# In an attention kernel's software pipeline, the look-ahead score products are issued first in each slot

## The chip, the cores and the metric

The kernel runs on one core of a Trainium2 chip. The metric is the time of one execution in microseconds (us), measured on the device. PE is TensorE (its weight loads are shown apart as PEld), DVE is VectorE, ACT is ScalarE, POOL is GpSimd, and SP issues the DMAs.

## The reference, cut to what matters

One layer of a bidirectional encoder is applied to two sequences, "prompt" (1024 tokens) and "sample" (2048 tokens), of width 1024. For each sequence:

```
h = rms_norm(x); z = h @ w_in            # split into pool, q, k, v, memory queries and gates
pool_out = multiscale_pool(u_pool) * silu(g_pool)
attn_out = softmax(q k^T / 8) v * silu(g_attn)       # 8 query heads, 2 key/value heads of 64, q and k normed and rotated
x_out    = softmax(q_x k_m^T / 8) v_m * silu(g_x)    # 4 heads on 256 memory tokens
y = concat(pool_out, attn_out, x_out) @ w_out
out = x + rms_norm(y)
```

All is float32. The softmax subtracts the largest score of each query. The inputs' gains make the scores large, so that the subtraction is needed.

## The kernel before, in words

The first part of the program (up to about 700 us) makes the projections and writes q, k, v and the gates to DRAM. The second part makes the attention and the output projection, and the change lies there.

The second part goes over **pairs** of 128 queries (256 queries): the eight pairs of the sample first, then the four of the prompt. A pair has three **groups**, one for each of the two key/value heads (kinds 0 and 1) and one for the memory attention (kind 2). A group goes over its keys in chunks of 128: 16 for a sample head, 8 for a prompt head, 2 for the memory. One chunk is one **slot**. A sample pair so has 34 slots and a prompt pair 18. The loop at line 877 issues slot after slot, and on PE, DVE, ACT and POOL the instructions stand in just the order in which the loop issues them.

What a slot holds:

- **Scores**, `weights(k, j)` for j = 0 and 1 (L220, L224 for kind 2): two matmuls make 128 keys by 512 queries into one of two PSUM buffers S, and ACT takes the exponential (L227) into P. The largest score comes in through an extra row of the second operand, `qb`.
- **Sums**, `sums(k)` of the slot before (L239, L240): P is added to z. In the sample POOL adds the first half and DVE the second; in the prompt DVE adds all.
- **The look-ahead**, `largest(n)`: for a group that comes later, two matmuls (four in kind 2, L183) make 128 queries by 1024 scores into one of two PSUM buffers N (L191), and DVE takes their largest (L194, `nb` or `top`). After the last piece of a group, `shift` turns the results into the row of `qb` (L201, L128, and DMAs at L161 and L209). There is nearly always one look-ahead in a slot; the last slots have none.
- **Due work** at dictated slots, `due(slot)` in the middle and `due(slot + 0.5)` at the end: the values matmuls (L252) once for every four chunks; after a group's last chunk its totals (L260), which take one of the two N buffers, then `take` (L266, `o`) and the reciprocal (L272, `rz`), which frees that buffer; then the product with the gate on POOL (L288), the split for the output projection (ACT and POOL, L416) and the norm of the output (L383 and L386).
- **Fill**: the matmuls of the output projection of an earlier pair (L357 to L359), spread over the middle slots of a sample pair and the last ones of a prompt pair.

Call the slot of a group's first chunk its first slot. The totals of the group before stand at the end of the slot after it, `take` and the reciprocal one slot further. The buffers of N are given out in the order in which they came free: while the totals hold one, the N of the next two slots share the other, and the N of the third one gets the buffer that the reciprocal frees. The buffers that are given out are the same ones before and after the change.

The order of a slot in the kernel before (L879 to L911) is: S(k, 0); sums of k-1; loads; look-ahead N; `due(slot)`; S(k, 1); fill; `due(slot + 0.5)`.

Of the kernel before, what the change touches and what calls it, by code (L numbers as in the profile page):

```python
# [23 lines left out]
def encoder(ctx, tc, I, O):  # L24
# [385 lines left out]
    def at(slot, f, *args):  # L410

        later.setdefault(slot, []).append((f, args))

    def due(slot):
        for f, args in later.pop(slot, ()):
            f(*args)  # L416
# [36 lines left out]
    looks, n = {}, len(slots)  # L453
# [421 lines left out]
    with tc.manual_schedule(engines=order):  # L875
        slot = 0
        while slot < len(slots) or later or fill:
            g, k = slots[slot] if slot < len(slots) else (None, 0)
            if g:  # L879
                g.weights(k, 0)  # L880
            if 0 < slot <= len(slots):
                h, kh = slots[slot - 1]
                h.sums(kh)
            for x in loads.get(slot, ()):
                x.load()
            if slot in looks:
                looks[slot][0].largest(looks[slot][1])
            due(slot)
            if g:
                g.weights(k, 1)  # L890
            pauses = sum(x is None for x in fill)
            n = -(-(len(fill) - pauses) // max(1, until[0] - slot - pauses)) if fill else 0
            for _ in range(n):
                x = fill.pop(0)
                if x is None:
                    break
                out, h, c, start, final = x
                out.piece(h, c, start, final)
                if final:
                    if h == 0 and not out.last:  # L900

                        for n in sorted(later):
                            for x in [x for x in later[n] if x[0].__name__ in ("square", "norm", "out")]:
                                later[n].remove(x)
                                x[0](*x[1])
                    at(slot + END, out.half_out, h)
                    at(slot + 1 + END, out.square, h)
                    if h == 1:
                        at(slot + 2, out.norm)
                        at(slot + 3, out.out)  # L910
            due(slot + END)  # L911
            slot += 1
# [42 lines left out]
```

## Time and profile before

| | |
|---|---|
| time, median of 3 runs | 1884.9 us (1884.27 to 1885.07) |
| the profiled execution | 1885.1 us, of which the span of the instructions is 1883.0 us |
| PE busy | 1816.8 us, 96% |
| DVE busy | 1131.4 us, 60% |
| POOL busy | 856.7 us, 45% |
| ACT busy | 697.3 us, 37% |
| mean granted clock of PE | 0.991 |

Each row of a timeline gives the start in us from the span's first instruction, how long the instruction (or the run of like ones, "x2") took, the engine, the line of the kernel, the operation, what it writes and reads, and in brackets the idle time of the engine before it with what ended it. A row of waits reads: who waited for whom, us in total, how many times, the longest. The ends of matmuls are modelled: a matmul is shown for about 0.4 us, while two matmuls of 512 columns that follow each other start about 0.235 us apart, so the idle time shown before a matmul is less than the time lost by about 0.16 us. In the rows of windows, the granted clock of PE (1.00 is full speed) stands in front of the DMA share.

### The profile page before, as it was taken

Reading aid. Unit: us, or ns where it says so; the run is one execution under the profiler, and the core shown is the slowest. Engines: PE = TensorE matmul, PEld = TensorE weight load, DVE = VectorE, ACT = ScalarE, POOL = GpSimd, SP = SyncE. Lnnn points to the kernel's source line nnn. Section 1 sums busy time; section 2 is a strip of 40 time slices with the busy share of each in tenths; the row PEclk is TensorE's granted clock in tenths of the full one; section 3 lists DMA queues with packets and bytes.
Section 4 is the critical chain, followed back from the end, with each engine's and each line's share of the span. In section 5 each row is a group of like instructions: output and inputs, shape, how many; then the busy total and the mean of one; then the engine's idle time right before and its main releaser. Section 6 shows DMA issues by size and latency. Waiting matters only on the chain. (4 is left out here: it accounts for less than half of the span.)

```text
span 1883.0 us, 23531 instructions
## 1 busy us (share of the span) xinstructions
PE 1816.8 (96%) x8520; PEld 1282.0 (68%) x8520; DVE 1131.4 (60%) x1304; ACT 697.3 (37%) x1266; POOL 856.7 (45%) x756
## 2 busy tenths in 40 slices
PE   7999999999999998999999999999999999999996
PEld 6888888988988874465564656556565656565564
DVE  7755146431545167867768676767868576756743
ACT  5523233222422115434434343444434343433331
POOL 3665017520546008845638374664837461413313
PEclk9999999999999999999999999999999999999998
DMA  7634454254433926212122220212222242223211
GB/s 243 201 113 121 109 160 132 76 162 110 116 113 102 216 70 167 68 30 79 46 79 62 70 64 25 79 45 79 62 74 62 67 132 64 91 84 100 86 40 62
DMA packets 148485, 181.83 MB, mean 97 GB/s; under 512 B 21505, under 2 KB 118417, under 8 KB 148369
## 3 DMA queue, kind: packets, MB, share of 16 engines
q1 hardware_dynamic: 148368, 180.33, 33.6%
q8 instruction: 67, 1.10, 0.3%
q14 instruction: 50, 0.40, 0.1%
HBM read 126.50 MB, written 53.62 MB: 96 GB/s over the span
## 5 line engine op out<-in xcount | busy, mean ns | idle before, releaser
L227 ACT ACTIVATE P<-S 128x512 f32<-128x512 f32 x688 | 399.3, 598 | 558.3 <-PE S L220 436.2
L194 DVE TENSOR_REDUCE nb<-N 128x1 f32<-128x1024 f32 x256 | 311.6, 1218 | 240.3 <-PE N L191 239.5
L239 POOL TENSOR_TENSOR z<-z,P 128x512 f32<-128x512 f32 x224 | 316.9, 1415 | 223.7 <-ACT P L227 218.8
L252 PE MATMUL acc<-P,V 128*64 128x512 f32 (+1 forms) x1472 | 320.8, 578 | 0.5
L220 PE MATMUL S<-qa,KA 128*128 128x512 f32 x640 | 275.0, 430 | 9.2 <-ACT P L227 9.2
L240 DVE TENSOR_TENSOR z<-z,P 128x512 f32<-128x512 f32 (+1 forms) x272 | 273.6, 1006 | 12.7 <-ACT P L227 12.3
L63 POOL TENSOR_TENSOR rs<-rs,mhalf 128x1 f32<-128x1 f32 (+2 forms) x100 | 100.4, 1007 | 386.2 <-DVE rs L61 386.1
L220 PE MATMUL S<-qb,KB 65*128 65x512 f32 x640 | 254.5, 398 | 0.0
L548 PE MATMUL pz<-hT_hi,w_hi 128*128 128x512 f32 x592 | 233.2, 394 | 1.4 <-ACT vmst L806 0.8
L549 PE MATMUL pz<-hT_lo,w_hi 128*128 128x512 f32 x592 | 232.3, 392 | 0.0
L550 PE MATMUL pz<-hT_hi,w_lo 128*128 128x512 f32 x592 | 232.1, 392 | 0.2 <-DVE w_lo L69 0.2
L191 PE MATMUL N<-KA,qa 128*128 128x512 f32 x640 | 208.1, 406 | 18.4 <-DVE rz L272 11.7
L252 PEld LDWEIGHTS acc<-P,V 128*64 128x64 f32 x1472 | 98.6, 138 | 180.3 <-issue 171.2
L220 PEld LDWEIGHTS S<-qa,KA 128*128 128x128 f32 x640 | 120.4, 188 | 143.6 <-issue 72.5
L194 DVE TENSOR_REDUCE top<-N 128x1 f32<-128x1024 f32 (+1 forms) x88 | 107.0, 1218 | 96.7 <-PE N L191 76.9
L191 PEld LDWEIGHTS N<-KA,qa 128*128 128x128 f32 x640 | 116.9, 191 | 61.7 <-DVE nb L194 22.1
L548 PE MATMUL pz<-w_hi,hT_hi 128*128 128x384 f32 (+1 forms) x416 | 140.3, 338 | 1.4 <-ACT hT_hi L68 1.4
L549 PE MATMUL pz<-w_lo,hT_hi 128*128 128x384 f32 (+1 forms) x416 | 139.9, 336 | 1.0 <-DVE w_lo L69 0.9
L550 PE MATMUL pz<-w_hi,hT_lo 128*128 128x384 f32 (+1 forms) x416 | 140.1, 338 | 0.0
L357 PE MATMUL py<-wo_hi,mix 128*128 128x512 f32 x352 | 137.7, 391 | 0.0
L358 PE MATMUL py<-wo_lo,mix 128*128 128x512 f32 x352 | 137.6, 391 | 0.0
L359 PE MATMUL py<-wo_hi,mix 128*128 128x512 f32 x352 | 137.4, 390 | 0.0
(116 smaller groups left out, 2487.9 us busy)
## 6 DMA issues: line engine op xcount, KB each, us to landing
wraw<-w_in SPq DMA_DIRECT2D x15, 1536.0 KB
dg<-gst SPq DMA_DIRECT2D x48, 256.0 KB
qa<-dq SPq DMA_DIRECT2D x48, 256.0 KB
gz<-rows SPq DMA_DIRECT2D x72, 128.0 KB
x<-x_sample SPq DMA_DIRECT2D x16, 512.0 KB
xr<-x_sample SPq DMA_DIRECT2D x16, 512.0 KB
y_sample<-xr SPq DMA_DIRECT2D x16, 512.0 KB
dq<-qst SPq DMA_DIRECT2D x96, 64.0 KB
```

The lines of the kernel that those rows point to most:

```text
L191: nc.tensor.matmul(S[:, 512 * b:512 * b + 512], lhsT=q, rhs=KA[self.kind][:, k:k + 512], start=True, stop=True)
L194: nc.vector.tensor_reduce(out=out, in_=S, axis=AX.X, op=ALU.max, negate=True)
L220: nc.tensor.matmul(S, lhsT=K[self.kind][rows_, keys], rhs=q, start=n == 0, stop=n == 1)
L227: nc.scalar.activation(out=self.P[k][:, j], in_=S, func=AF.Exp)
L239: nc.gpsimd.tensor_tensor(out=z[:, :cut], in0=a[:, :cut], in1=P[:, :cut], op=ALU.add)
L240: nc.vector.tensor_tensor(out=z[:, cut:], in0=a[:, cut:], in1=P[:, cut:], op=ALU.add)
L252: nc.tensor.matmul(self.acc[64 * j:64 * j + 64, x], lhsT=v, rhs=P[:, j, x], start=(k, i) == (0, 0), stop=k == self.chunks - 1, skip_group_ ...
L357: nc.tensor.matmul(ps, lhsT=mh, rhs=wo_hi[:, c, cols], start=first, stop=False)
L358: nc.tensor.matmul(ps, lhsT=mh, rhs=wo_lo[:, c, cols], start=False, stop=False)
L548: nc.tensor.matmul(ps, lhsT=sh, rhs=mh, start=c == 0, stop=False)
L549: nc.tensor.matmul(ps, lhsT=sh, rhs=ml, start=False, stop=False)
L550: nc.tensor.matmul(ps, lhsT=sl, rhs=mh, start=False, stop=c == n - 1)
```

## The change

The look-ahead of a slot is issued at the slot's start: on PE its matmuls (N) stand in front of S(k, 0), where they stood behind it; on DVE its maximum stands in front of the sum of weights of the slot before, where it stood behind it. With it moves what `largest` issues after a group's last piece (L201, L128 on DVE and the DMAs of `qb`), and the loads of the slot are issued behind it.

```diff
         while slot < len(slots) or later or fill:
             g, k = slots[slot] if slot < len(slots) else (None, 0)
+            if slot in looks:
+                looks[slot][0].largest(looks[slot][1])
             if g:
                 g.weights(k, 0)
             if 0 < slot <= len(slots):
                 h, kh = slots[slot - 1]
                 h.sums(kh)
             for x in loads.get(slot, ()):
                 x.load()
-            if slot in looks:
-                looks[slot][0].largest(looks[slot][1])
             due(slot)
             if g:
                 g.weights(k, 1)
```

The order on ACT and on POOL is the same in both kernels. On SP a few DMAs change places. PE at the start of a sample pair, from the totals (L260) to the values of the first four chunks, before:

```order
L260 MATMUL N<-z,ones 32x256 x4
L220 MATMUL S<-qa,KA_5426 128x512
L220 MATMUL S<-qb,KB_5427 128x512
L191 MATMUL N<-KA_5428,qa 128x512 x2
L220 MATMUL S<-qa,KA_5426 128x512
L220 MATMUL S<-qb,KB_5427 128x512
L220 MATMUL S<-qa,KA_5426 128x512
L220 MATMUL S<-qb,KB_5427 128x512
L191 MATMUL N<-KA_5428,qa 128x512 x2
```

The same place after, as far as the second N behind the totals:

```order
L260 MATMUL N<-z,ones 32x256 x4
L191 MATMUL N<-KA_5428,qa 128x512 x2
L220 MATMUL S<-qa,KA_5426 128x512
L220 MATMUL S<-qb,KB_5427 128x512
L220 MATMUL S<-qa,KA_5426 128x512
L220 MATMUL S<-qb,KB_5427 128x512
L191 MATMUL N<-KA_5428,qa 128x512 x2
```

In each slot N has moved in front of the pair of matmuls that makes S(k, 0); the two S of a slot are now neighbours. DVE at the same place before, from the maxima (L194) of the two slots around the totals to the sums behind the reciprocal:

```order
L240 TENSOR_TENSOR z<-z,P 128x512
L194 TENSOR_REDUCE nb<-N 128x1 x2
L240 TENSOR_TENSOR z<-P 128x512
L194 TENSOR_REDUCE nb<-N 128x1
L266 TENSOR_TENSOR o<-acc,gate 128x512
L272 RECIPROCAL rz<-N 128x256
L240 TENSOR_TENSOR z<-z,P 128x512
L194 TENSOR_REDUCE nb<-N 128x1
```

And after:

```order
L240 TENSOR_TENSOR z<-z,P 128x512
L194 TENSOR_REDUCE nb<-N 128x1 x2
L240 TENSOR_TENSOR z<-P 128x512
L266 TENSOR_TENSOR o<-acc,gate 128x512
L272 RECIPROCAL rz<-N 128x256
L194 TENSOR_REDUCE nb<-N 128x1
L240 TENSOR_TENSOR z<-z,P 128x512
```

The first sum of the new group (z<-P) stood between two maxima; it now stands behind both and directly in front of `o` and the reciprocal. PE at the end of a prompt pair's fill, before:

```order
L359 MATMUL py<-wo_hi,mix 128x512
L220 MATMUL S<-qa,KA_5428 128x512
L220 MATMUL S<-qb,KB_6119 128x512
L191 MATMUL N<-KA_5426,qa 128x512 x2
L220 MATMUL S<-qa,KA_5428 128x512
L220 MATMUL S<-qb,KB_6119 128x512
L220 MATMUL S<-qa,KA_5428 128x512
```

And after:

```order
L359 MATMUL py<-wo_hi,mix 128x512
L191 MATMUL N<-KA_5426,qa 128x512 x2
L220 MATMUL S<-qa,KA_5428 128x512
L220 MATMUL S<-qb,KB_6119 128x512
L220 MATMUL S<-qa,KA_5428 128x512
L220 MATMUL S<-qb,KB_6119 128x512
L191 MATMUL N<-KA_5428,qa 128x512 x2
```

The N of the second slot stood behind that slot's S(k, 0) and now stands in front of it.

## The prediction

> **What bounds the kernel now.** I read the page first: the busy shares and the clock row.
>
> ```profile
> PE 1816.8 (96%) x8520; PEld 1282.0 (68%) x8520; DVE 1131.4 (60%) x1304; ACT 697.3 (37%) x1266; POOL 856.7 (45%) x756
> ```
>
> PE is busy for 96% of the span, so the end is PE's own work plus the time it waits. The change adds and removes no instruction, so only the waits, and the clock that they may cost, can move. The second view is the list of waits of PE over the part where slots run, split at the start of the prompt's pairs (the first three rows are for 690 to 1530 us, the last two for 1530 to 1883 us).
>
> ```profile
> PE N L191 <- DVE nb L194: 5.8, 16, 1.0
> PE N L191 <- DVE rz L272: 5.2, 9, 0.6
> PE S L220 <- ACT P L227: 4.6, 18, 0.3
> ...
> PE N L191 <- DVE rz L272: 6.5, 4, 2.0
> PE S L220 <- ACT P L227: 4.6, 13, 0.5
> ```
>
> The reader is to see how little there is to win: 27 us in these five rows. The waits of N on rz (the reciprocal) come once at each pair's start. The third view is the timeline of one such start, in a sample pair, with PE, DVE, ACT and POOL (columns: start, duration, engine, line, idle time before).
>
> ```profile
> 1122.64 0.50 PE L220 MATMUL S<-qa,KA 128*128 128x512 f32 x1
> 1123.21 0.63 PE L191 MATMUL N<-KA,qa 128*128 128x512 f32 x2
> 1124.24 0.64 PE L260 MATMUL N<-z,ones 128*32 128x256 f32 x8
> 1124.81 0.50 PE L220 MATMUL S<-qa,KA 128*128 128x512 f32 x1
> 1125.02 0.94 DVE L240 TENSOR_TENSOR z<-P 128x512 f32<-128x512 f32 x1
> 1125.38 0.63 PE L191 MATMUL N<-KA,qa 128*128 128x512 f32 x2
> 1126.05 1.23 DVE L194 TENSOR_REDUCE nb<-N 128x1 f32<-128x1024 f32 x1
> 1127.19 0.68 DVE L266 TENSOR_TENSOR o<-acc,gate 128x512 f32<-128x512 f32 x1
> 1127.33 0.72 PE L191 MATMUL N<-KA,qa 128*128 128x512 f32 x2 [0.32 <-DVE nb L194]
> 1127.79 1.75 DVE L272 RECIPROCAL rz<-N 128x256 f32<-128x256 f32 x1
> 1128.35 0.40 PE L220 MATMUL S<-qa,KA 128*128 128x512 f32 x1
> 1129.59 0.73 PE L191 MATMUL N<-KA,qa 128*128 128x512 f32 x2 [0.61 <-DVE rz L272]
> 1130.72 3.65 PE L252 MATMUL acc<-P,V 128*64 128x512 f32 x16
> ```
>
> Call the slots from 1122.64, 1124.81, 1126.32 and 1128.35 one to four. The totals (L260) take one of the two N buffers; the N of slots two and three then share the other, and the N of slot four waits for rz. Before that N stands S(k, 0), which PE makes while it would else wait. And DVE adds z<-P at 1125.02 while it waits for the N of slot two: it costs rz nothing there.
>
> **The change part by part.** *Pair starts.* With N in front, N of slot one starts at 1122.64, and N of slot two right behind the totals at 1124.81, 0.57 earlier. Its reduction began 0.67 behind N (1125.38 to 1126.05); the first pair of matmuls after the totals takes 0.11 longer (1124.81 to 1125.38 for one S, against 0.47 for two matmuls elsewhere), so it begins at 1125.59 and ends at 1126.81. N of slot three can be issued at 1126.32 and waits till about 1126.86: 0.54, as before. But z<-P now stands behind this reduction and ahead of o and rz. Without a competitor it takes 0.68 (the middle value of the row below), so o ends near 1128.0 and rz at 1129.68 instead of 1129.54. N of slot four starts at 1129.73 and now has both S of its slot behind it, where it had one: the values start at 1131.33, not 1130.72. That is +0.6, with PE idle for about 0.38 and 1.20 us instead of 0.32 and 0.61. Nine such starts stand in the first list, and one of the four in the second: 10 x 0.6 = +6.0 us.
>
> How long z takes hangs on POOL, as these rows show (all sample z on DVE: least, middle and longest in ns; then one that starts while POOL adds xr).
>
> ```profile
> L240 DVE TENSOR_TENSOR z<-z,P x168: 627/683/1800, 802.2 to 1446.8; 128x512 f32<-128x512 f32 x168
> 1105.79 2.77 POOL L386 TENSOR_TENSOR xr<-xr,y 128x1024 f32<-128x1024 f32 x1 [1.17 <-DVE y L383]
> 1107.37 1.74 DVE L240 TENSOR_TENSOR z<-z,P 128x512 f32<-128x512 f32 x1
> 1126.37 1.28 POOL L239 TENSOR_TENSOR z<-z,P 128x512 f32<-128x512 f32 x1 [0.96 <-ACT P L227]
> ```
>
> A z that meets a running POOL sum waits it out: 1.74 is 1.2 of POOL's rest and 0.6 of its own. At a pair start POOL's next z begins after the exponential of slot two, by my count 0.1 us behind DVE's z<-P, so I take 0.68; if POOL comes first, it is up to 1.28 more (a rival).
>
> *The clock after a pair start.* Windows at the same place of an earlier sample pair, and at the end of a prompt pair and behind it (columns: length, busy of PE, PEld, DVE, ACT, POOL, then the granted clock and DMA).
>
> ```profile
> 1017.60:1021.10 3.50, 2.58 (x11) 1.58 (x10) 3.50 (x5) 2.11 (x4) 2.63 (x3) 1.00 0.25 74
> ...
> 1703.70:1707.10 3.40, 2.16 (x11) 1.21 (x9) 2.12 (x3) 2.17 (x4) 3.40 (x3) 1.00 0.50 172
> 1707.10:1714.00 6.90, 5.60 (x14) 2.29 (x16) 6.87 (x7) 0.60 (x2) 0.10 (x1) 0.51 0.47 147
> ```
>
> With 0.92 us of idle PE in 3.5 the clock stays at 1.00; with 1.24 in 3.4 it falls to half for 6.9. A pair start after the change has 0.38 + 1.20 = 1.58 us of idle PE spread over 3.2. I estimate that it falls below in 3 of 10, since the idle time often splits between two stretches; each then costs about 1.5 us (3.4 us at half the clock is 1.7 lost, less what falls in the wait): +4.5, between 0 and 15. The Trainium skill ("TensorE: Matmul & The Clock Gate", Part 1, on the clock gate) says the clock halves after at least one idle window of about 3.4 us. The row of 1703.70 speaks against reading this as a wholly idle window, since PE was busy for 2.16 of it; by the rule this term would be nothing.
>
> *Prompt pair ends.* There rz follows o, and o waits for POOL (DVE, POOL and PE).
>
> ```profile
> 1703.51 1.21 DVE L194 TENSOR_REDUCE top<-N 128x4 f32<-128x1024 f32 x1
> 1704.67 2.52 POOL L416 TENSOR_TENSOR mix<-o,mix 128x512 fp32r<-128x512 f32 x2
> 1705.99 0.69 DVE L266 TENSOR_TENSOR o<-acc,gate 128x512 f32<-128x512 f32 x1 [1.28 <-POOL mix L416]
> 1708.40 1.22 PE L191 MATMUL N<-KA,qa 128*128 128x512 f32 x2 [1.96 <-DVE rz L272]
> ```
>
> z<-P fits into DVE's idle 1.28, so rz stays; the S that stood ahead of N now stands behind it, 0.47 at the full clock or 0.94 at half: 0.7 each. Three such places (6.5 in four waits, the longest 2.0): +2.1; if z delays POOL's mix, up to 3.5 each.
>
> *Slots that wait for ACT.* PE waits for exponentials in two patterns: the end of a prompt fill (first two rows) and sample slots behind casts of mix (last two).
>
> ```profile
> 1676.37 0.40 PE L220 MATMUL S<-qa,KA 128*128 128x512 f32 x1
> 1678.47 0.50 PE L220 MATMUL S<-qa,KA 128*128 128x512 f32 x1 [0.55 <-ACT P L227]
> ...
> 1104.96 1.14 ACT L416 CAST mix<-o 128x512 fp32r<-128x512 f32 x2
> 1106.65 0.50 PE L220 MATMUL S<-qa,KA 128*128 128x512 f32 x1 [0.32 <-ACT P L227]
> ```
>
> In the first, S(k, 0) waits and N stands behind it, though its buffer is free; in front, its 0.47 fills the wait: six of the thirteen waits, -2.8. In the second, S(k, 1) waits; its S(k, 0) comes 0.47 later from PE, so ACT starts its queue up to 0.3 later: 8 x 0.3 = +2.4.
>
> *Plain sample slots.* A slot without fill, from its N to the S of the slot after next:
>
> ```profile
> 1134.88 0.63 PE L191 MATMUL N<-KA,qa 128*128 128x512 f32 x2
> 1135.35 0.40 PE L220 MATMUL S<-qa,KA 128*128 128x512 f32 x1
> 1135.82 0.47 PE L220 MATMUL S<-qa,KA 128*128 128x512 f32 x1
> 1137.28 0.47 PE L220 MATMUL S<-qa,KA 128*128 128x512 f32 x1
> ```
>
> The two matmuls of N take 0.47, so the six of a slot 1.41, and the pitch is 1.46: S(k, 0) waits 0.05 or a little more for the exponential two ahead of it. The two S are now neighbours, and the second exponential queues behind the first (1.14 for two casts of the same shape against 0.47 of PE between the two S), so the wait goes to S(k, 1) and about keeps its size; over a run of four slots I count 0.06 more: four runs in eight pairs, +2.0 (-2 to +4).
>
> *Slots where N waits for nb.* The first matmul of four such slots, and the values behind them:
>
> ```profile
> 1112.34 0.50 PE L220 MATMUL S<-qa,KA 128*128 128x512 f32 x1
> ...
> 1119.05 3.65 PE L252 MATMUL acc<-P,V 128*64 128x512 f32 x16
> ```
>
> The 5.8 us in 16 waits are a backlog of DVE. Each N comes 0.47 earlier, and with it each reduction, but as many z stand between two reductions as before: 0. Bounds: none of it goes away, or the four slots (6.71 us) shrink to their PE work, 4 x 1.41 and 0.20 at the two changes to and from values, 5.84: -0.87 in eight pairs, -7. The z of the slot before a burst of values now waits in DVE's queue behind an nb that waits for PE; nobody reads it before the next totals, so it costs 0 here.
>
> SP: some loads of qb's row stand earlier in its queue; no wait of PE above is on them: 0.
>
> Sum: 6.0 + 4.5 + 2.1 - 2.8 + 2.4 + 2.0 = +14.2 us. The profiled execution took 1885.1 (span 1883.0 and 2.1 around it), the median of the runs is 0.2 less: 1884.9 + 14.2 = 1899.
>
> **The rivals.** *No clock drop:* the threshold lies above 1.58 us of idle PE. The sum loses 4.5: 1894.6. For it: 0.92 left the clock alone, and the idle time is in two pieces; against it: 1.24 did not, and in pieces too. The clock-gate rule of the Trainium skill ("TensorE: Matmul & The Clock Gate", Part 1), cited above, would give this case.
>
> *POOL goes first, and every pair start halves the clock:* z<-P costs 1.28 more, the idle rises to 2.8 us, well past 1.24. 10 x (0.6 + 1.3 + 1.5) + 3.7 (the other terms) = 38: 1923. It decides from 0.1 us of DVE's order against POOL's.
>
> *Faster:* the earlier reductions dissolve DVE's backlog (-7.0), N fills ACT's waits (-2.8), the clock holds, the plain slots come out at their lower end (-2.0), and the pair starts' +6.0 stay: -5.8, 1879. It decides if nb of the first slot after each burst keeps its 0.47 lead through POOL's interference. For it: nb holds N up sixteen times in the first list; against it: the z left from before the burst comes right behind.
>
> *No change:* each wait only moves to another row, as the plain slots do: 1885.
>
> **How the numbers follow.** Forecast 0.42, no clock drop 0.18, POOL first 0.14, no change 0.14, faster 0.12. About 0.2%, 3.8 us, is what a measurement can tell here. Slower by more: 0.42 + 0.18 + 0.14 less 0.02 for forecasts that come out small = 0.72; same 0.16; faster 0.12. The range 1880 to 1912 takes in the first two cases with their bounds (prompt ends up to 3.5 each, plain slots -2 to +4) and no change; it leaves out most of faster and of POOL first, some 0.2 together.
>
> **What would show it.** In the changed profile: N waiting for rz in ten sample-like starts with about 1.2 idle instead of 0.6; z<-P right behind the second of two nb there, at 0.68; some stretches at clock 0.50 before 1530 us; fewer waits of S on P after the prompt's fills. I am wrong if the waits on rz do not grow, or if those on nb vanish.

## The result: slower, by more than forecast

| | before | after |
|---|---|---|
| median | 1884.99 us (4 runs) | 1916.64 us (4 runs, 1911.50 to 1924.97) |
| ratio, 95% interval | | 1.0166 [1.0144, 1.0187] |
| the profiled execution | 1885.1 us, span 1883.0 | 1924.97 us, span 1923.2 |

The change costs 31.7 us; 14 were forecast. The direction was right, the size too small, and 1917 lies above the range. The profiled execution of after is the longest of its four, 8 us over the median, so its rows show the places better than the total.

### The profile page after: what moved, and what is told of

It is laid out like the page before. It is cut to its first block, busy times and chain, and to the rows that moved or that the text cites. A ratio compares the mean times of both kernels' runs of the same rounds, so it can differ in the third digit from the quotient of the medians.

```text
span 1923.2 us, 23537 instructions
## 1 busy us (share of the span) xinstructions
PE 1834.4 (95%) x8520; PEld 1290.4 (67%) x8520; DVE 1144.6 (60%) x1304; ACT 679.0 (35%) x1266; POOL 875.5 (46%) x756
## 5 line engine op out<-in xcount | busy, mean ns | idle before, releaser
L227 ACT ACTIVATE P<-S 128x512 f32<-128x512 f32 x688 | 379.1, 597 | 615.2 <-PE S L220 263.8
L194 DVE TENSOR_REDUCE nb<-N 128x1 f32<-128x1024 f32 x256 | 311.1, 1216 | 252.5 <-PE N L191 252.1
L239 POOL TENSOR_TENSOR z<-z,P 128x512 f32<-128x512 f32 x224 | 350.4, 1564 | 229.1 <-ACT P L227 224.3
L252 PE MATMUL acc<-P,V 128*64 128x512 f32 (+1 forms) x1472 | 325.0, 585 | 1.5 <-DVE o L266 1.5
L220 PE MATMUL S<-qa,KA 128*128 128x512 f32 x640 | 267.1, 417 | 15.2 <-ACT P L227 14.8
L240 DVE TENSOR_TENSOR z<-z,P 128x512 f32<-128x512 f32 (+1 forms) x272 | 268.3, 986 | 11.1 <-ACT P L227 10.5
L63 POOL TENSOR_TENSOR rs<-rs,mhalf 128x1 f32<-128x1 f32 (+2 forms) x100 | 95.3, 956 | 389.6 <-DVE rs L61 389.6
L191 PE MATMUL N<-KA,qa 128*128 128x512 f32 x640 | 221.9, 428 | 28.4 <-DVE rz L272 17.7
L191 PEld LDWEIGHTS N<-KA,qa 128*128 128x128 f32 x640 | 108.3, 191 | 142.0 <-issue 61.9
L194 DVE TENSOR_REDUCE top<-N 128x1 f32<-128x1024 f32 (+1 forms) x88 | 107.2, 1218 | 116.3 <-PE N L191 86.8
L357 PE MATMUL py<-wo_hi,mix 128*128 128x512 f32 x352 | 137.9, 392 | 0.0
L220 PEld LDWEIGHTS S<-qb,KB 65*128 65x128 f32 x640 | 124.2, 194 | 20.0
```

The lines of the kernel that those rows point to most:

```text
L191: nc.tensor.matmul(S[:, 512 * b:512 * b + 512], lhsT=q, rhs=KA[self.kind][:, k:k + 512], start=True, stop=True)
L194: nc.vector.tensor_reduce(out=out, in_=S, axis=AX.X, op=ALU.max, negate=True)
L220: nc.tensor.matmul(S, lhsT=K[self.kind][rows_, keys], rhs=q, start=n == 0, stop=n == 1)
L227: nc.scalar.activation(out=self.P[k][:, j], in_=S, func=AF.Exp)
L239: nc.gpsimd.tensor_tensor(out=z[:, :cut], in0=a[:, :cut], in1=P[:, :cut], op=ALU.add)
L240: nc.vector.tensor_tensor(out=z[:, cut:], in0=a[:, cut:], in1=P[:, cut:], op=ALU.add)
```

## The profile after

The page's row of busy shares: PE has as many instructions as before, and 17.6 us more of busy time (1816.8 before), the same work, longer where the clock is lower (its mean is 0.983 in this execution and 0.991 in that of before).

```profile
PE 1834.4 (95%) x8520; PEld 1290.4 (67%) x8520; DVE 1144.6 (60%) x1304; ACT 679.0 (35%) x1266; POOL 875.5 (46%) x756
```

Waits of PE in the seven sample pairs between about 780 and 1550 us (total, times, longest), first before, then after:

```profile
PE N L191 <- DVE nb L194: 4.3, 13, 0.4
PE N L191 <- DVE rz L272: 4.2, 7, 0.6
PE S L220 <- ACT P L227: 4.2, 16, 0.3
```

```profile
PE N L191 <- DVE nb L194: 9.2, 24, 0.5
PE N L191 <- DVE rz L272: 8.4, 7, 1.2
PE S L220 <- ACT P L227: 7.6, 15, 0.8
PE acc L252 <- DVE o L266: 1.5, 6, 0.3
```

The reader is to see that all rows have grown, not the one on rz alone: nb by 4.9, rz by 4.2, ACT by 3.4, and a new one on `o`, 1.5: 14.0 us, 2.0 a pair. Now the prompt's pairs between 1570 and 1840 us, before and after:

```profile
PE N L191 <- DVE rz L272: 5.9, 3, 2.0
PE S L220 <- ACT P L227: 4.0, 11, 0.5
```

```profile
PE N L260 <- DVE z L240: 8.6, 3, 2.9
PE N L191 <- DVE rz L272: 6.9, 4, 1.7
PE S L220 <- ACT P L227: 2.4, 5, 0.7
```

The row that heads the second list was not forecast: at each of three prompt pair ends the totals wait 2.9 us for the last sum. First the place that was forecast, a sample pair's start, in the timeline of after:

```profile
1139.16 0.68 DVE L240 TENSOR_TENSOR z<-P 128x512 f32<-128x512 f32 x1
1139.27 1.72 POOL L239 TENSOR_TENSOR z<-z,P 128x512 f32<-128x512 f32 x1 [0.94 <-ACT P L227]
1139.30 0.73 PE L191 MATMUL N<-KA,qa 128*128 128x512 f32 x2 [0.38 <-DVE nb L194]
1139.76 0.68 DVE L266 TENSOR_TENSOR o<-acc,gate 128x512 f32<-128x512 f32 x1
...
1142.17 0.74 PE L191 MATMUL N<-KA,qa 128*128 128x512 f32 x2 [1.20 <-DVE rz L272]
```

The sum z<-P stands in front of `o` and is 0.11 us ahead of POOL's; PE waits 0.38 and 1.20, as forecast. And a prompt pair's end, which was not:

```profile
1652.39 2.29 DVE L383 SCALAR_TENSOR_TENSOR y<-y,rs,npost 128x1024 f32<-128x1024 f32 x1
1654.60 1.21 DVE L194 TENSOR_REDUCE top<-N 128x1 f32<-128x1024 f32 x1
1654.81 2.35 POOL L386 TENSOR_TENSOR xr<-xr,y 128x1024 f32<-128x1024 f32 x1 [1.22 <-ACT P L227]
1655.73 2.51 DVE L240 TENSOR_TENSOR z<-z,P 128x1024 f32<-128x1024 f32 x1
1658.39 1.08 PE L260 MATMUL N<-z,ones 128*32 128x256 f32 x8 [2.86 <-DVE z L240]
```

DVE is late by the product of the norm (L383); the maximum then goes first, and the last sum, which the totals need, comes behind it and runs beside POOL for 2.51 us instead of 1.2. The windows of after (length, busy of PE, PEld, DVE, ACT, POOL, then the granted clock and DMA): the first inside a sample pair, behind waits of 0.79 us on ACT and 0.46 on nb, the others around this prompt end:

```profile
1231.70:1235.10 3.40, 3.40 (x10) 1.29 (x10) 3.33 (x4) 1.20 (x2) 3.40 (x4) 0.50 0.38 154
1655.00:1658.40 3.40, 0.54 (x4) 0.14 (x4) 3.40 (x3) 0.91 (x2) 3.40 (x2) 0.99 0.11 47
1658.40:1661.70 3.30, 3.30 (x15) 2.21 (x16) 1.98 (x2) 0.15 (x1) 3.30 (x3) 0.50 0.50 187
1665.20:1672.00 6.80, 6.63 (x16) 3.06 (x18) 4.78 (x6) 1.19 (x2) 1.27 (x1) 0.50 0.21 65
```

PE is idle for 2.9 us at the prompt's pair end, and then has half the clock, twice.

## The experiments

Two questions: where does the loss sit, and what makes it? Theory A was the prediction's own: DVE's moved sum at the pair ends and starts, the idle time of PE that it makes, and the clock. Rival B: N in front on PE makes the loss everywhere. In the table each median stands beside that of the kernel before on the same chip; "both" are the two halves of the change. The ratio is that of the means of the runs.

| run | median | before | ratio, 95% interval |
|---|---|---|---|
| 1 PE's half alone | 1907.41 | 1884.59 | 1.0128 [1.0112, 1.0144] |
| 2 DVE's half alone | 1928.18 | 1884.59 | 1.0228 [1.0212, 1.0244] |
| 3 both, in the sample only | 1907.48 | 1884.59 | 1.0120 [1.0100, 1.0139] |
| 4 both, a group's last sum first | 1913.30 | 1884.59 | 1.0161 [1.0142, 1.0180] |
| 5 both, first and last sum first | 1911.01 | 1886.13 | 1.0142 [1.0122, 1.0163] |
| 6 both, PE kept busy | 1908.44 | 1884.29 | 1.0130 [1.0115, 1.0145] |
| 7 before, PE kept busy at three prompt ends | 1876.22 | 1884.29 | 0.9963 [0.9948, 0.9977] |
| 8 both, old order at the prompt's pair ends | 1914.61 | 1884.29 | 1.0152 [1.0132, 1.0173] |
| 9 both, old order at all pair ends | 1901.67 | 1884.29 | 1.0094 [1.0079, 1.0110] |
| 10 before, kept busy at more places, one of them wrong | 1879.29 | 1886.13 | 0.9970 [0.9958, 0.9983] |
| 11 as 9, DVE's half only | 1912.04 | 1886.13 | 1.0141 [1.0124, 1.0157] |
| 12 as 9, PE's half only | 1901.54 | 1886.13 | 1.0082 [1.0066, 1.0099] |
| 13 as 12, N behind S after values | 1898.18 | 1884.22 | 1.0071 [1.0054, 1.0088] |
| 14 as 11, sum in front of `o` | 1889.84 | 1884.22 | 1.0033 [1.0022, 1.0044] |
| 15 before, kept busy, place mended | 1874.91 | 1884.22 | 0.9951 [0.9940, 0.9963] |
| 16 as 9, casts late | 1898.60 | 1884.90 | 1.0075 [1.0063, 1.0087] |
| 17 as 16, sum in front of `o` | 1901.44 | 1884.90 | 1.0083 [1.0069, 1.0096] |
| 18 before, casts late | 1886.11 | 1884.90 | 1.0003 [0.9993, 1.0013] |

### Each half alone (1, 2), and the sample alone (3)

In run 1 `largest` is split into its matmuls and, as `maximum`, the reduction and what follows, and only the matmuls move. Run 2 puts the whole call behind S(k, 0) and in front of the sum, so that on PE the order stays and on DVE the reduction moves. Both are shown against the kernel before:

```diff
 # run 1
+            if slot in looks:
+                look = looks[slot][0].largest(looks[slot][1])
             if g:
                 g.weights(k, 0)
...
             if slot in looks:
-                looks[slot][0].largest(looks[slot][1])
+                looks[slot][0].maximum(*look)
             due(slot)
 # run 2
             if g:
                 g.weights(k, 0)
+            if slot in looks:
+                looks[slot][0].largest(looks[slot][1])
             if 0 < slot <= len(slots):
...
-            if slot in looks:
-                looks[slot][0].largest(looks[slot][1])
             due(slot)
```

Run 3 makes the change only in slots that belong to a sample pair.

> Only PE's half of the change: the N matmuls in front of S(k, 0), while DVE keeps the sum of weights in front of the maximum. Theory A (DVE's half does most: the first sum of a group delays the reciprocal, and the last sum of a group delays the totals in the prompt): the totals of the prompt pairs no longer wait, the reciprocal at pair starts ends as in the kernel before, and only the S that now stands behind N costs, about 0.4 at ten pair starts, with the slots that wait for ACT: 1890 to 1900 us. Theory B (PE's half does most: N at the head of the slot blocks both S behind it): near the changed kernel, 1910 to 1918.

> Only DVE's half: the maximum in front of the sum of weights of the slot before, PE's order as in the kernel before. Theory A: most of the loss stays, with totals of the prompt pairs that wait for the last sum (about 3 us idle in each of three places) and half the clock behind them: 1903 to 1915 us. Theory B: close to the kernel before, 1885 to 1892.

> The whole change, but only in the slots of the eight sample pairs; the prompt's slots are issued as before. By the alignment of slots in the two traces a sample pair loses 2.4 us without a fall of the clock and about 1.6 more with one; theory A: 8 x 2.4 and two or three falls, 1905 to 1910 us. If the prompt pairs carry most of the loss (a rival), under 1900.

Run 1 fell between the theories, run 2 above both: +22.8 and +43.6 us, where the two together cost 31.7. The halves do not add. Alone, DVE's half is the worse one, and N in front makes it milder; why was not tested (PE's waits on rz and `o` in the seven sample pairs are 15.2 us in run 2 and 9.9 in the changed kernel). As the only cause theory B falls, but PE's half alone costs 22.8 us, and DVE's half on top of it only 9 more. Run 3 came as expected: 22.9 us of the loss are the sample's, which leaves some 9 to the prompt.

### One sum back in front (4), two (5)

```diff
+            h, kh = slots[slot - 1] if 0 < slot <= len(slots) else (None, 0)
+            ahead_sum = h is not None and (kh == h.chunks - 1)    # run 5: (kh == h.chunks - 1 or kh == 1)
+            if ahead_sum:
+                h.sums(kh)
             if slot in looks:
                 looks[slot][0].largest(looks[slot][1])
...
-            if 0 < slot <= len(slots):
-                h, kh = slots[slot - 1]
+            if h is not None and not ahead_sum:
                 h.sums(kh)
```

> The changed kernel, but the sum of a group's last chunk is issued in front of the maximum, so that the totals do not wait for it behind that maximum. Theory A: the wait of the totals on DVE's last sum (10.0 us idle in four places of the changed kernel) goes, and with it the half clock behind it; about 12 us less than the changed kernel: 1902 to 1908 us. Rival (the wait moves on to the reciprocal, which is late for POOL's sake anyway): less than 4 us less, 1912 to 1918.

> The changed kernel, but on DVE the sum of a group's first two chunks and the sum of its last chunk stand in front of the maximum again, as before; PE's order is the changed one. Theory A (at a sample pair's start the loss is the sum that stands between the second maximum and the reciprocal): the N that waits for rz waits 0.6 instead of 1.2 us, about 6 us come back, and the half clock behind the pair starts goes: 1903 to 1910 us. Theory B (with N in front on PE the wait only passes to the N of the slot before, which waits for its maximum, as the run with PE's part alone showed with 0.8 there): 1909 to 1916, as with the last sum alone in front.

Run 4 stayed with the rival. Its waits of PE behind 1530 us, and DVE at a prompt pair's end:

```profile
PE N L260 <- DVE top L194: 4.4, 3, 1.5
```

```profile
1648.35 1.21 DVE L240 TENSOR_TENSOR z<-z,P 128x1024 f32<-128x1024 f32 x1
...
1649.48 2.34 DVE L194 TENSOR_REDUCE top<-N 128x1 f32<-128x1024 f32 x2
...
1650.75 0.64 PE L260 MATMUL N<-z,ones 128*32 128x256 f32 x8 [1.47 <-DVE top L194]
```

The time is in the rival's range, though not by its wait: that on rz hardly changes (6.9 to 6.7 us in all). The sum is early now, and the totals wait for the buffer that the maxima free, up to 1.5 us where they waited 2.9 for the sum. Changing the order of the last two alone halves the wait and gives it another name. The rest may come of the sums that stood over from the slots before, which leave DVE an operation behind; that was not tested. Run 5, with the first sum in front too, followed its theory B. Its waits in the sample:

```profile
PE N L191 <- DVE nb L194: 14.2, 23, 1.2
...
PE N L191 <- DVE rz L272: 4.2, 7, 0.6
```

What the pair starts no longer lose to rz (8.4 to 4.2) they lose to nb (9.2 to 14.2).

### The order of before at the pair ends (8, 9)

```diff
+    behind = set()
+    for n, pair in enumerate(pairs[:-1]):
+        if 8 <= n < 99:                              # run 9: if 0 <= n < 99
+            end = max(first[g] + g.chunks for g in pair.groups)
+            behind.update(range(end + -1, end + 5))
...
-            if slot in looks:
+            if slot in looks and slot not in behind:
                 looks[slot][0].largest(looks[slot][1])
...
                 x.load()
+            if slot in looks and slot in behind:
+                looks[slot][0].largest(looks[slot][1])
             due(slot)
```

> The changed kernel, but with the order of before (on PE and DVE) in six slots around the end of each pair from the ninth on: the last slot of the pair and the five behind it. Theory A (the prompt loses because at a pair's end the moved sum stands behind a maximum that waits for PE, and with the product of the norm and POOL's additions comes too late for the totals; a matter of these slots alone): the totals no longer wait 2.9 us, the clock falls less there, and 3 x 3.2 us and some of the half clock come back: 1901 to 1907. Theory B (DVE runs late through the whole prompt since N stands in front): the totals go on waiting, 1911 to 1918.

> As the run before, but in these six slots of all pairs, the sample's too. Theory A (the loss of the change sits at the pair ends and starts: 0.6 us and the halved clock at each sample start, the totals in the prompt; what is left are about 1.1 us in each sample pair in the slots before its end and behind the casts): 1890 to 1898 us. Theory B (the loss is spread over the slots; a slot that waits less hands its loss on): 1900 to 1912.

What is left of the totals' waits between 1570 and 1840 us in run 8, in the list of waits:

```profile
PE N L260 <- DVE top L194: 1.0, 3, 0.3
```

The 2.9 us are gone (0.3 at the longest), as theory A of run 8 has it. Its time is less plain: the profiled run took 1907.06, the edge of A's range, the three others 1914.16 to 1915.38, B's, with a mean clock of 0.991 and 0.986. So how much these three places return can't be read from it. Run 9, in all pairs, is clear: 17.4 us above before. Some 14 of the 31.7 us sit in six of the 34 (or 18) slots of a pair, and the rest, 17, elsewhere: theory A's 1890 to 1898 is missed by 4 us, B's range holds it.

### What is left: each half inside the pairs (11, 12), and its cause (13, 14)

Runs 11 and 12 are run 9 with one half each in the other slots. Run 14 adds to 11, and run 13 to 12, one line:

```diff
 # run 14: the slot of each group's take
+    behind.update(n + g.chunks + 2 for g, n in first.items())
 # run 13: the first slot behind each burst of values
+    behind.update(n for n, (g, k) in enumerate(slots) if k % RUN == 1)
```

> Outside the six slots around each pair's end only DVE's half of the change (maximum in front of the sum); in these six slots, and on PE everywhere, the order of before. Theory A (what is left of the loss with the old order at the pair ends, 17 us, comes from PE's half: the two S of a slot are neighbours, and the second one waits for an exponential behind the casts of mix and behind the values): 1885 to 1890 us. Theory B (it comes from DVE's half): 1896 to 1904.

> The counterpart: outside the six slots around each pair's end only PE's half (N in front of the scores); in these six slots, and on DVE everywhere, the order of before. Theory A (PE's half makes what is left): 1896 to 1903 us, as with both halves. Theory B (DVE's half makes it): 1885 to 1890.

> The run with DVE's half alone outside the pair ends (1912.0 us, 26 above the kernel before), but in the slot of each group's take (o) the sum stands in front of the maximum again. Theory A (in the sample, o of the memory group is made a sum later, and the values that wait for its accumulator lose 0.7 us): in each of eight sample pairs 0.7 us comes back, and PE no longer waits 4.5 us in all on o; the prompt's loss, which goes by the product of the norm and POOL to ACT, stays: 1904 to 1909 us. Theory B (the wait on o only replaced another one): 1910 to 1914.

> The run with PE's half alone outside the pair ends (1901.5 us, 15 above the kernel before), but in the first slot behind each burst of values N stands behind S(k, 0) again. Theory A (PE's half loses because, behind a burst, ACT gets its first exponential 0.45 us later, the time of N's two matmuls, and has no slack to make it up in the four slots of a run once casts of mix stand between the exponentials): the waits on ACT shrink to those of before, and the loss of some 1.2 us in each sample pair goes: 1886 to 1892 us. Theory B (the loss comes of N in front in any slot, since the two S are neighbours everywhere): 1896 to 1903.

Theory A on runs 11 and 12 was right on the second and wrong on the first, which lies above both of its ranges: DVE's half alone costs 25.9 us there, PE's half 15.4, both 17.4. Two places in the profile of run 11 say how. The first stands in its list of waits in the sample; the others are a timeline in the prompt.

```profile
PE acc L252 <- DVE o L266: 4.5, 6, 0.8
```

```profile
1612.32 1.23 DVE L194 TENSOR_REDUCE top<-N 128x1 f32<-128x1024 f32 x1 [0.93 <-PE N L191]
1613.46 1.22 DVE L240 TENSOR_TENSOR z<-P 128x1024 f32<-128x1024 f32 x1
1614.60 0.68 DVE L266 TENSOR_TENSOR o<-acc,gate 128x512 f32<-128x512 f32 x1
...
1617.61 2.38 POOL L386 TENSOR_TENSOR xr<-xr,y 128x1024 f32<-128x1024 f32 x1 [1.45 <-issue]
...
1620.03 0.59 ACT L365 COPY y<-py 128x512 f32<-128x512 f32 x1 [6.65 <-POOL xr L386]
...
1621.16 0.50 PE L220 MATMUL S<-qa,KA 128*128 128x512 f32 x1 [1.54 <-ACT P L227]
```

DVE stands idle 0.93 us for N, with a sum queued behind; then the sum takes its 1.2 us in front of `o` and of the norm's product (L383), POOL's addition comes late, ACT's copy of y waits for that, an exponential stands behind the copy, and PE waits 1.54 us for it. In the sample the values wait for `o` itself (0.8). Run 14 puts the sum back in front in this slot alone: 1889.84, at least 14 us below what theory A forecast, which had counted on the sample's place only; both are mended. There the sum runs in the time in which DVE waits:

```profile
1601.48 1.22 DVE L240 TENSOR_TENSOR z<-P 128x1024 f32<-128x1024 f32 x1
1602.62 1.22 DVE L194 TENSOR_REDUCE top<-N 128x1 f32<-128x1024 f32 x1
1603.75 0.68 DVE L266 TENSOR_TENSOR o<-acc,gate 128x512 f32<-128x512 f32 x1
```

So nearly all that DVE's half costs alone is located: with the old order at the pair ends and in this slot 5.6 us are left of the 43.6 of run 2.

PE's half is not. Run 13, 1898.18 us (1893.22 to 1903.29), lies in theory B's range, and its interval overlaps that of run 12; the waits on ACT stayed at 7.3 us in 15, where run 12 has 7.5 and before 4.2, so a late first exponential behind the values is not their cause.

### The casts (16, 17, 18)

```diff
-        at(slot + 1 + END, nc.scalar.copy, hi, a)
+        at(int(slot + END) + 1 + END, nc.scalar.copy, hi, a)
```

> The changed kernel with the old order in six slots around each pair's end (1901.7 us, 17 above the kernel before), and on ACT the casts of the attention's products (mix<-o) stand behind a slot's second exponential, where they stood between its two. Theory C (with N in front, the two S of a slot and so their exponentials are neighbours, and ACT's gap lies behind the second one; a cast between the two has no gap to fall into, which makes the waits on ACT of 10.2 us against 4.2 before): some 0.4 us comes back at each such cast, two in a sample pair, and the waits on ACT fall towards 5: 1893 to 1898 us. Theory D (ACT lacks time for the cast wherever it stands): 1900 to 1904.

> As the run before, and also the old order in the slot of each group's take. Both halves of the change stay in the other slots. Theory C, with the sum standing in front of o again: another 1.5 us of waits on o and some 0.5 us in each prompt pair come back: 1888 to 1895 us. If it gets below the kernel before, N in front is worth something in plain slots; theory C gives no reason for that.

> The kernel before with only these casts moved behind the slot's second exponential. Theory C: with N between the two S, the gap lies between the two exponentials, so the move takes the cast out of its gap and costs 0.2 to 0.4 us at some of sixteen places in the sample: 1886 to 1891. Theory D: the place of the cast does not matter: 1882 to 1886.

Waits of PE between 780 and 1550 us in run 9, then in run 16:

```profile
PE S L220 <- ACT P L227: 9.4, 22, 0.8
PE N L191 <- DVE nb L194: 8.7, 24, 0.4
```

```profile
PE N L191 <- DVE nb L194: 14.3, 22, 1.5
...
PE S L220 <- ACT P L227: 2.7, 9, 0.7
```

The waits on ACT do go with the casts' place (9.4 to 2.7), but 5.6 of those 6.7 us come back as waits for nb, and the time hardly moves (1901.67 to 1898.60). That is a little above theory C's range and below D's. Run 17, with `o` mended too, is no better and misses its range: the waits on `o` (1.6 us in run 16) are gone, and those on nb have grown from 14.3 to 16.9. In the order of before the place of the casts makes no difference that can be measured (run 18, interval across 1; its median lies where the two ranges meet). A slot that waits less for ACT hands its loss to N.

One place shows this row by row: in a sample pair, the four slots ahead of the last values of the second head. PE's waits there in the kernel before, in run 12 (whose line numbers from the reduction on are three higher) and in run 16:

```profile
1214.23 0.50 PE L220 MATMUL S<-qa,KA 128*128 128x512 f32 x1 [0.22 <-ACT P L227]
...
1215.75 0.50 PE L220 MATMUL S<-qa,KA 128*128 128x512 f32 x1 [0.32 <-ACT P L227]
```

```profile
1228.19 0.50 PE L223 MATMUL S<-qa,KA 128*128 128x512 f32 x1 [0.79 <-ACT P L230]
...
1229.31 0.73 PE L191 MATMUL N<-KA,qa 128*128 128x512 f32 x2 [0.38 <-DVE nb L197]
```

```profile
1226.55 0.73 PE L191 MATMUL N<-KA,qa 128*128 128x512 f32 x2 [1.48 <-DVE nb L194]
```

From values to values these slots take 10.57 us before (1207.28 to 1217.85), 11.25 in run 12 (1219.66 to 1230.91) and 11.30 in run 16 (1216.83 to 1228.13). The place of the casts decides whom PE waits for; the 0.7 us are lost either way. In the other six sample pairs from the second on run 12 takes 11.2 to 12.3 us there and the kernel before 10.6. What makes PE's half cost some 15 us inside the pairs stays open; the runs show only that it is no single one of these waits.

### PE kept busy while it waits (6, 7, 10, 15)

Matmuls into a PSUM tile that nobody reads, ahead of an instruction that would wait (run 7; run 6 has them in the changed kernel, five at seven sample starts, and twelve and seven at the prompt's ends):

```diff
+    idle = {}
+
+    def keep_busy(count):
+        pad = pso.tile([128, 512], F32, name="py", tag="py")
+        for _ in range(count):
+            nc.tensor.matmul(pad, lhsT=wo_hi[:, 0, 0:128], rhs=wo_hi[:, 1, 0:512], start=True, stop=True)
+
+    for pair in pairs[8:-1]:
+        end = max(first[g] + g.chunks for g in pair.groups)
+        idle[end + 3], idle[end + 4] = 2, 8
...
+            if slot in idle:
+                keep_busy(idle[slot])
             if slot in looks:
```

> The changed kernel with matmuls that nobody reads (five ahead of the N that waits for rz in seven sample pair starts; twelve ahead of the totals and seven ahead of that N at the prompt's pair ends), 0.235 us each, put where PE would stand idle, so that it is busy while it waits. No output changes. Theory A (part of the loss is the halved clock, and the clock halves because PE stands idle for more than about 1.2 us in 3.4): the stretches at half clock behind these places are gone, and with them 1.7 us for each of some three in the sample and up to 3.4 us for each of the prompt's; 1898 to 1908 us. Theory B (the clock falls by something else, or the waits alone make the loss): the stretches stay and the time is that of the changed kernel or a little more, 1912 to 1920.

> The kernel before with two and eight such matmuls ahead of N in the two slots of three prompt pair ends in which N waits for rz (2.0 us each). No output changes. Theory A (the idle PE halves the clock for 6.8 us there, which costs up to 3.4 us each): 1874 to 1881 us, faster than the kernel before. Theory B (the matmuls only push the work behind them): 1885 to 1892.

> The kernel before with the unread matmuls of the earlier run at three prompt pair ends, and further ones at the three other places where PE stands idle and the clock then halves: thirteen ahead of the first totals of the program (3.3 us of waiting), six ahead of the last totals and seven ahead of the last output projection. No output changes. Theory A (idle PE is what halves the clock): no stretch at half clock is left between 740 us and the last matmul; against the run with the first three places another 3.4 us at the first and 1.7 us at the tail are saved: 1869 to 1874 us. Theory B: the first and the last places are held up by transfers and POOL anyway, 1875 to 1878.

> The kernel before with the unread matmuls at three prompt pair ends and at the tail, and thirteen now ahead of the totals that wait 3.3 us for POOL at 753 us (the earlier run had put them ahead of the first totals of the program, where PE does not wait, so they cost 3 us there). No output changes. Theory A (idle PE halves the clock): no half clock is left between 740 us and the last matmul: 1870 to 1875 us. Theory B (POOL holds the totals, and the work behind them, anyway): 1875 to 1878.

Run 7 at a prompt pair end, timeline and window; the prediction shows the same place of before, with 1.96 us of waiting and a clock of 0.51 behind it:

```profile
1703.99 2.00 PE L880 MATMUL py<-wo_hi 128*128 128x512 f32 x8
1706.11 0.72 PE L191 MATMUL N<-KA,qa 128*128 128x512 f32 x2
```

```profile
1703.00:1710.00 7.00, 6.88 (x32) 3.86 (x33) 6.26 (x7) 1.69 (x3) 1.92 (x2) 1.00 0.44 153
```

N starts 7.0 us behind the totals of the group before it, as in the kernel before, and the clock holds: theory A, and 7 to 8 us under the kernel before (by the means and by the medians). Run 6 shows the same in the changed kernel: at a prompt pair's end the totals still come late, but at full clock,

```profile
1646.00:1653.00 7.00, 6.28 (x33) 4.18 (x32) 6.18 (x4) 2.28 (x4) 5.78 (x4) 1.00 0.18 75
```

and the ratio is 1.0130 against 1.0166 of the changed kernel (the median is 0.4 us above theory A's range): filling the waits returns some 7 us. That is not the clock's share of the 31.7. The same remedy returns as much in the kernel before, whose clock falls too, and on one chip the two filled kernels are 32.2 us apart (1908.44 and 1876.22), no less than the two unfilled ones. How much of the 31.7 us comes from added falls of the clock stays open. In run 10, which lies above both of its ranges, thirteen of these matmuls stood ahead of the wrong totals, where PE does not wait; in the trace the work behind them comes 3 us later, which is their own time (13 x 0.235). In run 15 they stand where PE waits 3.3 us for POOL: 1874.91, in theory A's range and the fastest of all the kernels, though against run 7 the intervals overlap.

## Why the prediction was wrong

- **The failed step: the slots inside the pairs.** The prediction gave them +2.0 (plain slots), 0 (slots that wait for nb), -2.8 and +2.4 (waits on ACT), 1.6 us together. With the old order at all pair ends they cost 17.4 (run 9), and this is nearly the whole miss: the pair ends got 12.6 with the clock, and run 9 returns 14.3. Inside the pairs PE's half alone costs 15.4 (run 12). N now stands in front of both S of its slot, and PE's waits for nb in the seven sample pairs go from 4.3 to 9.7 us, outside the bounds that the prediction gave them, nothing and -7; those on ACT go from 4.2 to 7.5. The two rows make 8.7 of the 15.4; why they grow so, and the rest, stay open.
- **A second wrong step** is a sentence: "The z of the slot before a burst of values now waits in DVE's queue behind an nb that waits for PE; nobody reads it before the next totals, so it costs 0 here." At a prompt pair's end the totals read such a sum at once, and everywhere what stands behind it in DVE's queue comes later: `o`, the product of the norm. The prediction saw this at the pair starts, where a sum that had run in DVE's idle time now stood in front of rz, and did not look for it at every other place where DVE waits for N. Two of these are shown. The prompt's totals wait 2.9 us each in the changed kernel. The slot of each take makes 20 us of what DVE's half costs alone (runs 11 and 14); in the changed kernel PE waits on `o` for 1.5 us in all, and taking such waits away returned nothing (run 17).
- **Pair starts, +6.0: right.** 1.2 us instead of 0.6 at rz, 0.38 at nb, z<-P at 0.68 ahead of POOL. With the order of before there (run 9) the waits on rz are those of before.
- **The clock, +4.5: right in its mechanism; its size is not settled.** Behind three of the ten starts it halves, as forecast: from 917.6 and 1477.4 us on for 3.4 each, and at the first prompt pair from 1586.7 for 6.8. The prediction has no term for falls inside the sample pairs (1231.70) or at the prompt's ends, where half the clock lasts 3.4 and then 6.8 us at each of three, against 3.4, 6.8 and 6.8 before. Runs 6 and 7 do not say what the added falls cost. The rival without a clock drop falls with the falls behind these starts, and so does the rule of the Trainium skill ("TensorE: Matmul & The Clock Gate", Part 1) if its idle window is read as a wholly idle one: the waits that were filled in run 7 were 2.0 us long. The rival in which POOL comes first falls with the 0.11 us above and with 1.2 us as the longest wait on rz in the sample.
- **Prompt pair ends, +2.1: wrong place.** What was forecast there, an S behind N, can hardly be seen (rz, longest wait 1.7 instead of 2.0); the loss comes before it, at the totals.
- **Waits on ACT: right in kind.** In the prompt -1.6 (4.0 to 2.4) where -2.8 was forecast, in the sample +3.4 where +2.4 was.

## What to carry to other kernels

An operation that waits for another engine should not stand in front of one whose operands are ready, if something behind both is waited for: list every place where the engine now waits, and follow the queue behind it to the next reader, through other engines too. A move on two queues should be costed for each queue by itself and at each kind of place; here the halves cost 23 and 44 us and both together 32. Where PE waits for a fixed time that can't be removed, work that nobody reads can be worth it, because the clock holds behind it (run 7).

## What the runs showed of the hardware

- Keeping PE busy through three waits of 2 us at prompt pair ends took 7 to 8 us off a kernel of 1884 (run 7), with no useful instruction changed: the granted clock behind these places stayed at 1.00, where it had been 0.50 for 3.4 to 6.8 us.
- Such matmuls where PE does not wait cost their own time, 3 us for thirteen (run 10).
- The clock does not fall each time that PE waits so long: nine times PE waited 1.20 us for rz in the sample, and behind two of them it halved (after).
- A sum on DVE beside additions of POOL took 2.51 us (1655.73 in after) where a sum of this shape took 1.22 elsewhere (1613.46 in run 11), and PE waited 2.86 us for its end.
